# Windowed attention with unscaled probabilities: the softmax reciprocals travel through DRAM and multiply the outputs

## The chip, the core and the metric

The kernel runs on one core of one Trainium2 chip, in one launch. The metric is the device time of a run in microseconds (us), as the median of several runs; smaller is better. One execution was also recorded by the hardware profiler, and everything said of waits and durations comes from that recording. The engines are named as the profile names them: PE is the matrix engine (PEld its weight loads), DVE the vector engine, ACT the scalar engine, POOL the GpSimd engine, SP the engine that issues most of the DMA transfers. An engine works through its own instructions strictly in the order in which they stand; a small q behind a name (SPq) is its queue of issuing and waiting instructions. PSUM is the memory that PE writes its results to; SBUF is the working memory of all engines; DRAM is the large memory outside.

## What is computed

The program is two layers of a diffusion backbone over 512 latent tokens and 256 context tokens, with a model width of 1024. Layer 0 is the windowed attention that the change touches; layer 1 is a retention layer, and both are followed by a gated feed-forward network. Of layer 0, this matters here:

```python
s_ctx = einsum('bqkgd,bnkd->bkgqn', qb, k_c) * scale
s_loc = einsum('bqkgd,bnkd->bkgqn', qb, kb) * scale
s_loc = where(valid, s_loc, NEG_INF)
p = softmax(concatenate([s_ctx, s_loc, sink_col], axis=-1))
o = einsum('bkgqn,bnkd->bqkgd', p[..., :L], v_c) + einsum('bkgqn,bnkd->bqkgd', p[..., L:L + band], vb)
```

There are 16 query heads in 4 groups of 4; the heads of a group share their keys and values. A latent query of a block of 128 sees its own block, the neighbouring blocks and all context keys; a context query sees the 256 context keys. A learned sink logit for each head takes part in the softmax and has no value.

## The kernel before

The stage around the change works in blocks: one group g of four heads, one stream s (0 latent, 1 context) and 128 queries. There are four latent and two context blocks in a group, so 24 in all; the change touches the 18 of groups 0 to 2. They are counted here from 0 to 17 in the order in which the kernel writes them. In each of groups 0 and 1 the four latent blocks come first and then the two context blocks; in group 2 the two context blocks are the third and the sixth. So blocks 4, 5, 10, 11, 14 and 17 are context blocks. A context block has two tiles of 128 keys; a latent block has four (at the ends) or five.

A block goes through these steps:

- `score`, lines 685 to 729, for each of the four heads: PE multiplies queries and keys into PSUM (L710); DVE adds the mask, takes the running minimum and writes the result to an SBUF tile `pr` (L711). After each second head, DVE makes the bias (L717), ACT takes the two exponentials and gets their row sums beside them (L725 is the next step; the exponentials go through the helper at L101), and DVE takes the reciprocals of the two sums (L721). Then the probabilities are scaled by the reciprocals: of each pair, the first head on DVE (L727), the second on ACT (L725).
- `turn`, line 731: for each tile of keys PE transposes the four heads' probabilities into one PSUM bank (L736), and ACT or DVE in turn copies the bank to an SBUF tile `tt` (L738).
- `output`, line 743: PE multiplies values and `tt` (L750) into a PSUM bank, of which the block uses 256 columns: the two halves of the 128 partitions hold two heads each. For groups 0 to 2, DVE copies this result into an SBUF tile `res` (L765), and later work splits it into the two parts that the output projection reads. For group 3 the split reads the bank directly.

In the layout of the scores a query is a partition, and its sum is one number for each partition: a scaling along the free dimension is one operand. In the layout of the outputs a query is a column, and a partition is a channel of the head.

Between the blocks stand pieces of other work. `make_q(j)` (lines 559 to 639) projects the queries of heads 2j and 2j+1: 24 matmuls with 512 columns and 24 with 256 (L147 to L149), then norms (L617 and L620), rotations on DVE (L589 to L592), and for j from 2 to 6 eight DMAs on SP that spread the result over the partitions (L605). It is called after the second and the fourth block of groups 0 to 2, for the next group. The weights come in with DMAs on SP (L122) and are split by ACT (L164) and DVE (L165).

The order on each engine in this stage isn't written by hand. The program is handed to a scheduler, which plays it through with its own estimates of durations, DMAs included, and fixes an order on each engine, SP among them. So the changed source gives a changed order over the whole stage, and the order can be read from the built program before it has run. Where a tile's buffer is used again, the scheduler adds a wait for the earlier use.

Of the kernel before, what the change touches and what calls it, by code (L numbers as in the profile page):

```python
# [8 lines left out]
F32 = mybir.dt.float32  # L9
# [5 lines left out]
P = 128  # L15
# [6 lines left out]
NKV = 4  # L22
# [27 lines left out]
def dit_kernel(ctx, tc, xT, cT, crow, small, consts, masks, tabs0, tabs1, jtab, adaQ, adaN, adaT, wst, out):  # L50
    nc = tc.nc
    mult, add, sub = ALU.mult, ALU.add, ALU.subtract
# [6 lines left out]
    rp = ctx.enter_context(tc.tile_pool(name="rp", bufs=1, reuse_waits="tile"))  # L59
    psJ = ctx.enter_context(tc.tile_pool(name="psJ", bufs=1, reuse_waits="tile", space=PSUM))  # L60

    def T(pool, cols, tag, bufs, dt=F32):
        return pool.tile([P, cols], dt, tag=tag, bufs=bufs, name=tag)
# [36 lines left out]
    def lnexp(*args, **kw):  # L100
        ins = nc.scalar.activation(*args, **kw)  # L101
        after(ins, [turn["pre"]])
        turn["lnexp"].append(ins)
        return ins
# [58 lines left out]
    def split(t, hi, lo, behind=()):  # L163
        after(nc.scalar.copy(hi, t), behind)  # L164
        return nc.vector.tensor_tensor(lo, t, hi, op=sub)  # L165
# [66 lines left out]
    def h_tiles(s):  # L232
        hi = t_h(s)
        if s == 0:
            return hi, t_h(s)
        return hi[:, 0:SC], hi[:, SC:2 * SC]
# [47 lines left out]
    pO = lambda: T(psA, 512, "pO", 1)  # L284
# [234 lines left out]
    At = ExitStack()  # L519
    ap = At.enter_context(tc.tile_pool(name="ap", bufs=1, reuse_waits="tile"))  # L520
# [36 lines left out]
    q, stats = {}, {}  # L557
# [110 lines left out]
    psA2 = At.enter_context(tc.tile_pool(name="psA2", bufs=1, reuse_waits="tile", space=PSUM))  # L668
    pS = lambda: T(psA2, 512, "S2", 3)

    run_dep = mybir.DependencyInfo(mybir.DependencyClass.Sync, mybir.DependencyReason.DATA)
    o_raw = {}
    o_t = [[None] * KT, [None] * KT]

    class Block:


        def __init__(self, g, s, b):
            self.g, self.s, self.b = g, s, b
            self.lk = list(range(max(0, b - 1), min(4, b + 2))) if s == 0 else []  # L680
            ck = [4, 5]
            self.keys = ck + self.lk if s == 0 and b == 3 else self.lk + ck
            self.pr = []

        def score(self, i):
            g, s, b, n = self.g, self.s, self.b, len(self.keys) * P
            hd, nl = 4 * g + i, len(self.lk) * P
            if i % 2 == 0:
                self.st = T(ap, 16, "stat", 4)
            st, c = self.st, 2 * (b + 4 * s)  # L690
            qt = q[hd, s][:, b * P:(b + 1) * P]
            pt = T(ap, 656, "pr", PRB)[:, :n + 1]
            top = stats[hd][:, 1, c + hd % 2:c + hd % 2 + 1]
            nc.gpsimd.tensor_copy(pt[:, n:n + 1], top)
            lo, x0 = st[:, i % 2:i % 2 + 1], self.lk[0] * P if nl else 0

            if nl == 384:
                runs = [(nl, SC, 5 * P, [(0, SC, kc)]), (0, nl, 2 * P, [(0, nl, kx)])]
            elif nl == 0:
                runs = [(0, SC, 5 * P, [(0, SC, kc)])]  # L700
            elif b == 0:
                runs = [(0, n, 3 * P, [(0, nl, kx), (nl, SC, kc)])]
            else:
                runs = [(0, n, 0, [(0, SC, kc), (SC, nl, kx)])]
            for c0, w, m0, parts in runs:
                bank = pS()[:, :w]
                for p0, pw, kk in parts:
                    for r in range(2):
                        keys = kk[g][r] if kk is kc else kk[g][r][:, x0:x0 + pw]
                        nc.tensor.matmul(bank[:, p0:p0 + pw], qt, keys, start=r == 0, stop=r == 1)  # L710
                nc.vector.tensor_tensor_reduce(pt[:, c0:c0 + w], bank, mask[:, m0:m0 + w], 1.0, top, add, ALU.min, lo)  # L711
                top = lo
            self.pr.append(pt)
            if i % 2 == 0:
                return
            y = stats[hd][:, 0, c:c + 2]
            nc.vector.scalar_tensor_tensor(st[:, 2:4], st[:, 0:2], -1.0, y, mult, mult)  # L717
            for e in range(2):
                pt = self.pr[i - 1 + e]
                lnexp(pt, pt, AF.Exp, scale=y[:, e:e + 1], bias=st[:, 2 + e:3 + e], accum_out=st[:, 4 + e:5 + e])  # L720
            nc.vector.reciprocal(st[:, 6:8], st[:, 4:6])  # L721
            for e in range(2):
                pt = self.pr[i - 1 + e]
                if e:
                    nc.scalar.activation(pt[:, :n], pt[:, :n], AF.Identity, scale=st[:, 6 + e:7 + e])  # L725
                else:
                    nc.vector.tensor_scalar(pt[:, :n], pt[:, :n], st[:, 6 + e:7 + e], None, op0=mult)  # L727
            if i == 3:
                self.tt = []
# [12 lines left out]

        def output(self):
            g, s, b = self.g, self.s, self.b
            O = pO()[:, :256]
            for ki, (t, tt) in enumerate(zip(self.keys, self.tt)):
                vg = vt[t][:, g * HD:(g + 1) * HD]
                f, l = ki == 0, ki == len(self.keys) - 1
                for e in range(2):
                    ins = nc.tensor.matmul(O[64 * e:64 * e + 64, :], vg, tt[:, 256 * e:256 * e + 256], start=f, stop=l)  # L750
                    if f:
                        tc.add_manual_dep(ins.ins, self.last.ins.name, run_dep, reason="value products in one run")
            if g == NKV - 1:
                if b == 0:
                    for e in range(2):
                        o_t[s][2 * g + e] = h_tiles(s)
                for e in range(2):
                    hi, lo = o_t[s][2 * g + e]
                    cs = slice(b * P, b * P + P)
                    split(O[:, e * P:e * P + P], hi[:, cs], lo[:, cs])  # L760
                return
            if b % 2 == 0:
                o_raw[g, s, b // 2] = T(rp, 512, "res", 12)
            dst = o_raw[g, s, b // 2].rearrange("p (e b q) -> p e b q", e=2, b=2)[:, :, b % 2, :]
            nc.vector.tensor_copy(dst, O.rearrange("p (e q) -> p e q", e=2))  # L765

    def attend(g, s, b):
        blk = Block(g, s, b)
# [377 lines left out]
    for gsz in FFN_GROUPS:  # L1146
        acts = []
        made[:] = 0, gsz
        for i in range(gsz):
            if f < PLAIN:  # L1150
                acts.append(first[f])
                if f == 1:
                    ends.pop(0)()
            else:
                if f == PLAIN:
                    last_sum()
                a, end = seven()
                acts.append(a)
                if f == PLAIN:
                    ends.pop(0)()  # L1160
                if f == 4:
                    cr = cond_rows(fp)
                if f > 3 and (i or f == 6):
                    ada_next(end)
            if i == 0 and prev is not None:
                output(prev, False)
            f += 1
        prev = acts
# [4 lines left out]
    hpool[0] = H.enter_context(tc.tile_pool(name="hR", bufs=1, reuse_waits="tile", side="right"))  # L1173
    wsel[0] = 0
    output(prev, True)
    F.close()
    E.close()
# [24 lines left out]
    def chunk(i, own=False):  # L1202
        raw = T(qw, 1024, "wx", 4) if own else T(rp, 1024, "wraw", 2)
        nc.sync.dma_start(raw, wst[i])
        return raw
# [156 lines left out]
    for hd in range(RH):  # L1362
# [26 lines left out]
        halves = lambda o: enumerate((o[:, 0:SC], o[:, SC:2 * SC]))  # L1389
# [145 lines left out]
        for i in range(2):  # L1535
            g, v = chunk(bg + i), chunk(bv + i)
# [259 lines left out]
    for gsz in FFN_GROUPS:  # L1796
        acts = []
        for i in range(gsz):
            if f < 2:
                acts.append(first[f])  # L1800
            elif f == 2:
                w = [next_w(fp, behind=norm_end) for _ in range(2)]
                token_sums(hm, 3, sh2, sA, [weights_end])
                other_parts()
                acts.append(plain(w))
            else:
                acts.append(seven(late))
            late = output(prev, False) if i == 0 and prev is not None else ()
            f += 1
        prev = acts  # L1810
# [146 lines left out]
```

## Time and profile before

| | us |
|---|---|
| median of 3 runs (1734.84 to 1737.31) | 1736.23 |
| the profiled execution's own time | 1732.25 |
| its span, first to last instruction | 1730.3 |
| first and last matmul of the scores (L710), from the span's start | 99.5 and 301.8 |
| first and last copy of an output to `res` (L765) | 119.6 and 268.8 |

The profile's page has the busy time of each engine, the span in slices, the chain of work that ended last (followed back from the last instruction, at each step to what released it), groups of equal instructions, and the DMAs. A row of a group says how often it occurs, its busy time and its mean, and the idle time of its engine just before it with what ended that idle time. A row of the stretches gives the busy time of every engine in a part of the span. A row of the timeline gives start, duration, engine, line, operation, and the tiles written and read. A busy PE isn't a PE at its peak, because matmuls overlap each other.

### The profile page before, as it was taken

The page shows a single profiled execution, that of the slowest core. Times are in us where ns is not written, and L with a number is a line of the kernel's source. Part 1 is how long each engine was busy: PE and PEld are TensorE (multiplying, and loading weights), DVE is VectorE, ACT ScalarE, POOL GpSimd, SP SyncE. Part 2 cuts the span into 40 slices and gives each one's busy share as a digit, 9 for nine tenths or more (in the row PEclk, how much of TensorE's full clock was granted, in tenths as well). Part 3 has the DMA queues.
Part 4 walks back from the last instruction along what each step waited for, and adds up shares of the span by engine and source line. Part 5 has one row for each costly group of instructions (what it writes and reads, how often), then busy time and mean ns, then how long its engine had stood idle before and what let it go on. Part 6 is the DMA issues. An engine that isn't in the chain of part 4 may idle for free.

```text
span 1730.3 us, 27786 instructions
## 1 busy us (share of the span) xinstructions
PE 1698.0 (98%) x10876; PEld 1513.0 (87%) x10876; DVE 1361.0 (79%) x2436; ACT 871.1 (50%) x1552; POOL 50.5 (3%) x168
## 2 busy tenths in 40 slices
PE   7999999999999999999999999999999999999999
PEld 5788877899999999999988788898897899899998
DVE  6698889798778788787889858858758798877874
ACT  5587779465433334342556534524525464445442
POOL 0000000000000000000000000000000000000000
PEclk9999999999999999999999999999999999999999
DMA  9612221543253434343423524523423223333322
GB/s 349 239 30 57 62 62 56 209 134 121 73 157 117 153 110 148 123 154 102 156 99 88 183 77 132 163 82 124 159 90 108 95 74 103 117 102 116 100 86 86
DMA packets 62803, 207.48 MB, mean 120 GB/s; under 512 B 7248, under 2 KB 8912, under 8 KB 62416
## 3 DMA queue, kind: packets, MB, share of 16 engines
q1 hardware_dynamic: 55184, 178.97, 32.0%
q0 software_dynamic: 7200, 26.22, 5.2%
q8 instruction: 85, 1.39, 0.3%
q10 hardware_dynamic: 288, 0.52, 0.1%
q14 instruction: 46, 0.38, 0.1%
HBM read 199.65 MB, written 2.10 MB: 117 GB/s over the span
## 4 chain that ended last, share of the span: by engine, by line
PE 78%; DVE 11%; DMA 6%; ACT 3%; issue 2%; SPq 0%; ACTq 0%; DVEq 0%
PE Y L897 14%; PE pj L147 7%; PE Z L897 7%; PE pj L149 7%; PE pj L148 7%; PE Z L1292 6%; PE X L897 3%; DMA wraw<-in_wst_dram 3%; PE pT L736 2%; PE pO L750 2%; PE S L710 2%; DVE wlo L165 2%; PE Y L1281 2%; PE pj L1292 2%; PE X L1281 1%
## 5 line engine op out<-in xcount | busy, mean ns | idle before, releaser
L164 ACT CAST whi<-wraw 128x1024 fp32r<-128x1024 f32 x258 | 270.0, 1051 | 333.7 <-PE Z L149 81.9
L165 DVE TENSOR_TENSOR wlo<-wraw,whi 128x1024 fp32r<-128x1024 f32 x258 | 314.3, 1221 | 64.5 <-ACT whi L164 62.7
L897 PE MATMUL Y<-aq,whi 128*128 128x384 f32 x640 | 173.5, 335 | 0.6 <-ACT hn L1053 0.6
L897 PEld LDWEIGHTS Y<-aq,whi 128*128 128x128 f32 x640 | 116.6, 188 | 1.6 <-ACT hn L1053 1.4
L256 DVE SCALAR_TENSOR_TENSOR res<-pj,mod,res 128x512 f32<-128x512 f32 (+1 forms) x112 | 81.0, 728 | 41.5 <-PE pj L149 41.2
L897 PE MATMUL Y<-aq,wlo 128*128 128x384 f32 x320 | 107.0, 334 | 0.0
L273 DVE CUSTOM_DVE_ANT_0 y<-adaw,crow,small_sb 128x1024 bf16<-128x1024 f32 x64 | 81.9, 1280 | 29.6 <-DMA adaw<-in_adaT_dram 29.4
L1292 PE MATMUL Z<-whi,sA 128*128 128x512 f32 x256 | 81.7, 394 | 1.4 <-ACT gate L1478 1.4
L101 ACT ACTIVATE pr<-pr,stat,qs 128x513 f32<-128x513 f32 (+2 forms) x96 | 74.2, 775 | 9.1 <-DVE stat L717 8.8
L147 PE MATMUL pj<-ax,whi 128*128 128x512 f32 x176 | 69.0, 392 | 1.2 <-DVE res L256 1.2
L149 PE MATMUL pj<-ax,whi 128*128 128x512 f32 x176 | 68.6, 390 | 0.0
L148 PE MATMUL pj<-ax,wlo 128*128 128x512 f32 x176 | 68.6, 390 | 0.0
L147 PE MATMUL pj<-act,whi 128*128 128x512 f32 x168 | 65.6, 391 | 0.0
L148 PE MATMUL pj<-act,wlo 128*128 128x512 f32 x168 | 65.5, 390 | 0.0
L149 PE MATMUL pj<-act,whi 128*128 128x512 f32 x168 | 65.5, 391 | 0.0
L897 PEld LDWEIGHTS Y<-aq,wlo 128*128 128x128 f32 x320 | 60.1, 188 | 0.0
L1292 PEld LDWEIGHTS Z<-whi,sA 128*128 128x128 f32 x256 | 48.0, 188 | 13.0 <-ACT gate L1478 2.6
L711 DVE CUSTOM_DVE_ANT_0 pr<-S,mask,qs 128x256 f32<-128x256 f32 (+1 forms) x96 | 53.1, 566 | 7.8 <-PE S L710 5.3
L897 PE MATMUL Y<-sA,whi 128*128 128x256 f32 x304 | 58.1, 277 | 0.6 <-ACT res L1746 0.6
L897 PE MATMUL Y<-hx,whi 128*128 128x256 f32 x304 | 56.3, 277 | 0.0
L736 PE MATMUL pT<-const_sb,pr 128*128 128x128 f32 x352 | 53.6, 278 | 1.5 <-ACT tt L738 0.9
L1292 PE MATMUL Z<-wlo,sA 128*128 128x512 f32 x128 | 50.7, 396 | 0.2
(581 smaller groups left out, 5070.4 us busy)
## 6 DMA issues: line engine op xcount, KB each, us to landing
wraw<-in_wst_dram SPq DMA_DIRECT2D x224, 512.0 KB, 3.6
adaw<-in_adaT_dram POOLq DMA_DIRECT2D x48, 512.0 KB, 3.9
wx<-in_wst_dram SPq DMA_DIRECT2D x30, 512.0 KB, 4.3
adan<-in_adaQ_dram SPq DMA_DIRECT2D x16, 512.0 KB, 8.8
adan<-in_adaN_dram SPq DMA_DIRECT2D x12, 512.0 KB, 7.7
adaw<-in_adaT_dram SPq DMA_DIRECT2D x8, 512.0 KB, 3.9
res<-in_xT_dram SPq DMA_DIRECT2D x14, 256.0 KB, 3.2
aq<-in_adaN_dram SPq DMA_DIRECT2D x12, 256.0 KB, 5.7
```

The source lines that it names most:

```text
L101: ins = nc.scalar.activation(*args, **kw)
L147: nc.tensor.matmul(o, whi, xhi, start=first, stop=False)
L148: nc.tensor.matmul(o, wlo, xhi, start=False, stop=False)
L149: return nc.tensor.matmul(o, whi, xlo, start=False, stop=last)
L164: after(nc.scalar.copy(hi, t), behind)
L165: return nc.vector.tensor_tensor(lo, t, hi, op=sub)
L256: return nc.vector.scalar_tensor_tensor(res[d], o, mods[l, s][:, part, d:d + 1], res[d], mult, add)
L273: res.append(nc.vector.tensor_tensor_reduce(junk, w, cr[:, s * 1024:(s + 1) * 1024], 1.0, sm_t[:, C_ADAB + l * 48 + j:C_ADAB + l * 48 + j ...
L711: nc.vector.tensor_tensor_reduce(pt[:, c0:c0 + w], bank, mask[:, m0:m0 + w], 1.0, top, add, ALU.min, lo)
L736: nc.tensor.transpose(tp[:, a * P:(a + 1) * P], self.pr[(0, 2, 1, 3)[a]][:, ki * P:(ki + 1) * P], ident)
L897: nc.tensor.matmul(o, p, r, start=first and k + i == 0, stop=k == 3 and i == 2, skip_group_check=not first)
L1292: ins = nc.tensor.matmul(os[t], p, r, start=first and k + i == 0, stop=k == 3 and i == 2, skip_group_check=by_k or not first)
```

## The change

For groups 0 to 2 the probabilities stay unscaled. The two reciprocals of each pair of heads are written by a DMA on SP from the `stat` tile (128 partitions with two numbers each) to a tile of two rows in DRAM: 256 pieces of four bytes. When the second pair of a block has been written, two more DMAs on SP read each row, of 256 numbers, to 64 partitions each: a tile `factor` with a row for every partition. Its buffer alternates between a new one and one that stood unused in this stage (`y1`). The copy of the block's output (L765 before) becomes a product with `factor` (L781 after). The outputs of all blocks now share one PSUM bank, taken once, and blocks of groups 0 to 2 use its two halves in turn. Group 3 is computed as before.

```diff
+    o_bank, o_count = pO(), [0]
+    rows = At.enter_context(tc.tile_pool(name="rows", bufs=1, reuse_waits="tile", space=bass.MemoryType.DRAM))
...
+            self.factor = None
+            if g < NKV - 1:
+                self.row = rows.tile([2, 256], F32, tag="row", bufs=4, name="row")
...
             nc.vector.reciprocal(st[:, 6:8], st[:, 4:6])
+            if g < NKV - 1:
+                nc.sync.dma_start(self.row[:, i // 2 * P:(i // 2 + 1) * P].rearrange("e q -> q e"), st[:, 6:8])
+                if i == 3:
+                    o_count[0] += 1
+                    self.factor = T(ap, 256, "factor", 1) if o_count[0] % 2 else T(rp, 256, "y1", 1)
+                    for e in range(2):
+                        nc.sync.dma_start(self.factor[64 * e:64 * e + 64, :], self.row[e:e + 1, :].broadcast_to([64, 256]))
+                    self.tt = []
+                return
             for e in range(2):
...
-            O = pO()[:, :256]
+            c0 = 0 if self.factor is None else 256 * (o_count[0] % 2)
+            O = o_bank[:, c0:c0 + 256]
...
-            nc.vector.tensor_copy(dst, O.rearrange("p (e q) -> p e q", e=2))
+            halves = [t.rearrange("p (e q) -> p e q", e=2) for t in (O, self.factor)]
+            nc.vector.tensor_tensor(dst, *halves, op=mult)
```

In the changed program the lines behind the insertions move: the reciprocal is L726, the writes of the rows are L728, the reads L733, the remaining scaling of group 3 L740 and L742, the transposes L750, the copies to `tt` L752, the value products L765 and the product with `factor` L781.

## The prediction

> **What bounds the kernel now.** The page was read first. The matrix engine is busy nearly throughout, so a saving counts only where PE waits.
>
> ```profile
> span 1730.3 us, 27786 instructions
> PE 1698.0 (98%) x10876; PEld 1513.0 (87%) x10876; DVE 1361.0 (79%) x2436; ACT 871.1 (50%) x1552; POOL 50.5 (3%) x168
> ```
>
> The change works between 112 us (first scaling of the second pair of heads) and 269 us (last copy of an output). I cut that time into three stretches, by what the chain of waits does in them. Each row gives start and end, length, then busy time and count of PE, PEld, DVE, ACT and POOL, the granted clock, and the DMAs.
>
> ```profile
> 112.00:121.00 9.00, 7.92 (x53) 5.46 (x53) 8.77 (x32) 8.11 (x17) 1.01 (x4) 1.00 0.00 0
> 121.00:247.00 126.00, 124.75 (x903) 102.65 (x902) 102.68 (x338) 98.31 (x221) 10.57 (x60) 1.00 0.24 64
> 247.00:265.00 18.00, 13.46 (x91) 10.43 (x93) 14.60 (x51) 13.99 (x36) 0.55 (x4) 0.91 0.11 31
> ```
>
> In the first, DVE is busy for 8.77 of 9 us. In the long middle PE is busy for 124.75 of 126, and DVE and ACT are idle for 23 and 28 us. In the third, PE is busy for only 13.46 of 18, and its clock was 0.91. The chain, cut to the same stretches, agrees:
>
> ```profile
> by line: DVE pr L711 26.7%; DVE tt L738 14.0%; DVE pr L727 9.6%; PE S L710 9.6%; DVE y L589 8.1%; DVE hn L590 6.7%; DVE y L591 6.7%; DVE hn L592 6.7%; PE pj L617 6.2%; DVE res L765 3.7%; DVE stat L721 0.8%; issue 0.7%; DVE stat L717 0.6%; D
> by line: PE pT L736 20.6%; PE S L710 19.6%; PE pO L750 19.2%; PE pj L147 11.6%; PE pj L149 11.1%; PE pj L148 11.1%; PE pj L617 4.6%; issue 1.2%; ACT tt L738 0.9%; DVE pr L711 0.2%; DVE stat L711 0.2%; DVE hn L165 0.0%; DVEq L711 0.0%
> by line: PE pO L750 20.8%; DVE pr L711 18.5%; ACT pr L101 12.0%; PE S L710 7.3%; DVE q L610 6.2%; PE pT L736 5.5%; issue 4.1%; ACT q L608 3.5%; ACT pr L725 3.4%; PE pj L617 3.1%; ACT qs L101 2.8%; ACT tt L738 2.6%; DVE q L609 2.3%; DVE stat
> ```
>
> DVE sets the first, PE alone the middle, and DVE and ACT in turn the third, where no projections are left to fill PE.
>
> **What is removed.** 36 scalings on DVE and 36 on ACT go (18 blocks, four heads). The groups hold 37 of each, because one pair of group 3 falls into the same time.
>
> ```profile
> L725 ACT ACTIVATE pr<-pr,stat 128x256 f32<-128x256 f32 (+2 forms) x37 | 25.0, 678 | 5.3 <-DVE stat L721 4.4 <-DVE stat L717 0.8
> L727 DVE TENSOR_SCALAR pr<-pr,stat 128x256 f32<-128x256 f32 (+2 forms) x37 | 16.9, 457 | 0.3
> L765 DVE COPY res<-pO 128x256 f32<-128x256 f32 x18 | 7.6, 420 | 4.8 <-PE pO L750 4.7
> ```
>
> That is some 16.5 us of DVE and 24.3 us of ACT, most of it in the middle, where PE covers it. By stretch (length, busy time, count), first the scalings on DVE, then those on ACT:
>
> ```profile
> 112.00:121.00 9.00, 1.05 (x3) 1.00 0.00 0
> 247.00:265.00 18.00, 1.66 (x4) 0.91 0.11 31
> 112.00:121.00 9.00, 1.85 (x3) 1.00 0.00 0
> 247.00:265.00 18.00, 2.42 (x4) 0.91 0.11 31
> ```
>
> First stretch: the chain holds 9.6% of 9 us of L727, 0.87 us; DVE is full, so I take 1.0, with bounds of 0.87 and ACT's 1.85. Third stretch: the chain holds 3.4% of 18 us of L725, 0.6 us; the exponentials queue behind these scalings too, so I take 2.0, between 0.6 and 2.4. Middle: of its chain, 2.5% isn't PE (1.2 + 0.9 + 0.2 + 0.2), 3.1 us; I take 0.7, between 0 and 3.1, since the rows name no scaling there.
>
> **What is moved.** The scheduler's new order moves one costly thing into another place: the split of a weight tile at the head of the third stretch.
>
> ```profile
> 249.48 1.23 DVE L165 TENSOR_TENSOR wlo<-wraw,whi 128x1024 fp32r<-128x1024 f32 x1 [0.28 <-ACT whi L164]
> 254.50 0.47 PE L710 MATMUL S<-kc,q 128*128 128x256 f32 x2 [2.53 <-DVE qs L620]
> 259.48 0.71 ACT L725 ACTIVATE pr<-pr,stat 128x512 f32<-128x512 f32 x1
> 259.85 0.85 PE L736 MATMUL pT<-const_sb,pr 128*128 128x128 f32 x6 [0.47 <-DVE pr L727]
> ```
>
> It stood ahead of the chain that PE awaits for 2.53 us; now it stands behind that, between a reciprocal and a copy to `tt`, where it delays something else by the same 1.23 us. The clock row (0.91 of 18 us) says that up to 1.6 us of PE time went to a lowered clock there. I take a gain of 0.5, between 0 and 1.6. Sum of gains: 1.0 + 2.0 + 0.7 + 0.5 = 4.2 us; bounds 1.5 and 9.0.
>
> **What is added.** The product in place of the copy reads the same 256 columns of PSUM and one SBUF tile more. No row shows it in that form; it stands between nothing added and the copy's own 0.42 us once more, 18 times, off PE: 0 taken. SP gets 36 writes and 36 reads. Its nearest transfers are those of the queries:
>
> ```profile
> L605 SPq DMA_DIRECT2D q<-y x20: 461/538/598, 120.8 to 233.3; - x20
> L605 SPq DMA_DIRECT2D q<-hn x20: 462/587/1467, 122.1 to 234.6; - x20
> DMA to landing us min/median/max: 1.9/2.3/4.2
> q<-hn SPq DMA_DIRECT2D x10, 64.0 KB, 2.9
> out_dram<-res SPq DMA_DIRECT2D x8, 256.0 KB, 2.0
> ```
>
> An issue holds SP for about 0.55 us, so 72 of them hold it for 40 us of 157, which costs nothing by itself. The path that counts is from a block's second reciprocal to its product: write and landing, then two reads one behind the other: 2.3 + 0.55 + 2.3 = 5.1 us by the medians, 1.9 + 0.55 + 1.9 = 4.4 by the fastest, 4.2 + 0.55 + 4.2 = 9.0 by the slowest. The 64 KB reads are like the row with 2.9; for the write of four-byte pieces I take 2.9 as well: 6.3 us.
>
> What covers it? From the second reciprocal over the scaling to the copy, for blocks 0, 5 and 7:
>
> ```profile
> 112.59 0.16 DVE L721 RECIPROCAL stat<-stat 128x2 f32<-128x2 f32 x1
> 113.58 0.48 DVE L727 TENSOR_SCALAR pr<-pr,stat 128x512 f32<-128x512 f32 x1
> 119.64 0.42 DVE L765 COPY res<-pO 128x256 f32<-128x256 f32 x1
> 157.29 0.16 DVE L721 RECIPROCAL stat<-stat 128x2 f32<-128x2 f32 x1
> 158.29 0.50 ACT L725 ACTIVATE pr<-pr,stat 128x256 f32<-128x256 f32 x1
> 161.97 0.42 DVE L765 COPY res<-pO 128x256 f32<-128x256 f32 x1
> 170.77 0.16 DVE L721 RECIPROCAL stat<-stat 128x2 f32<-128x2 f32 x1
> 171.43 0.55 DVE L727 TENSOR_SCALAR pr<-pr,stat 128x640 f32<-128x640 f32 x1
> 180.71 0.41 DVE L765 COPY res<-pO 128x256 f32<-128x256 f32 x1
> ```
>
> So 6.9, 4.5 and 9.8 us pass, of which the scaling takes 1.0 to 1.3. Without it, latent blocks still have 5.6 to 8.7 us until their value products end, but context blocks only 3.2 to 4.1. The new order helps these: ahead of each product it puts other DVE work, which I counted from the order and these means:
>
> ```profile
> L711 DVE CUSTOM_DVE_ANT_0 pr<-S,mask,qs 128x256 f32<-128x256 f32 (+1 forms) x79 | 43.9, 569 | 6.7 <-PE S L710 5.3 <-POOL pr L694 0.5 <-PE pT L736 0.3
> L738 DVE COPY tt<-pT 128x512 f32<-128x512 f32 x30 | 20.7, 689 | 8.3 <-PE pT L736 8.0
> ```
>
> Block 0 has 6.4 us of it (five score reductions, two copies, three rotations of 0.7 and small ones), context blocks 5.6 to 8.0. The larger of the two covers, over the 18 blocks, is 5.6 to 8.7 us, mean 7.0. At 6.3 us only blocks 10, 11, 12 and 14 fall short, by 2.0 us together; the DVE queue stands for that long, and the score reductions and copies behind it, for which PE waits. DVE's idle time takes up part: I book 0.4, with 0 at 5.1 us. The 9.0 us end is rival B.
>
> **The sum.** 4.2 − 0.4 = 3.8 us less. Against the profiled execution's own 1732.25 us (1.95 around the span) that is 1728.5; the median of the runs stands 4.0 above that execution, so the forecast is 1736.2 − 3.8 = **1732.4 us**.
>
> **Rival A is the forecast; B: the factors come late (slower).** The place is L781 at the head of DVE's queue. From the covers above, a path of 7 us lacks 6.4 us in all 18 blocks, of 8 us 18, of 9 us 35. With half of it reaching PE, the gain of 4.2 is eaten at about 7.2 us; at 9 us the time is 1736.2 + 17.7 − 4.2 = 1750. For it: no row has a write of four-byte pieces, and SP waits in its own queue for each row's landing before the reads. Against it: the copies to `tt` that PE needs first stand ahead of the product in most blocks. The Trainium skill (DMA: Bandwidth & Descriptors, Rules for kernel authors and Specifications) says that a strided last dimension becomes one descriptor per element, and that under 512 bytes the engine reads, changes and writes back; by that rule the write is the slow kind, and B is the likelier for it. No run here shows it yet.
>
> A second mechanism makes B dearer: in the new order the value products of block 5 wait for the product of block 4, although they use different halves of the bank, so a late factor also holds PE directly. The Trainium skill (PSUM — Partial Sum Buffer, PSUM bank collisions raise a hardware error) says that two engines may not use one bank at once, by which two halves of a bank are no double buffer; the order agrees.
>
> **C: no change.** The third stretch is ruled by the exponentials and score reductions themselves, so only the chain's own pieces go (0.87 + 0.6 = 1.5), and the 2.0 us of shortfall reach PE in full: 1736.2 − 1.5 + 2.0 = 1736.7. For it: the chain names little of L725 and nothing in the middle.
>
> **D: the queries come late (slower).** The transfers of the next group's queries stand on SP behind reads that wait for a landing. If each of the five projections that use them is held for a landing and two issues, 2.3 + 1.1 = 3.4 us, and a third of it shows: 1736.2 + 5.7 = 1742 with no gain left. Against it: the order puts these transfers where their sources are only just made.
>
> **How the numbers follow.** A 0.45, B 0.21, C 0.24, D 0.10. The bound of a measurable difference is 0.2%, 3.5 us. A gives faster, C the same, B and D slower: 0.45, 0.24, 0.31. A alone reaches from 1736.2 − 9.0 = 1727 to the edge at 1733; the range adds B's end above and a little for a reordered stage below: 1725 to 1750.
>
> **What would show it.** Right: the first and third stretch shorter by 1 and 2 to 3 us, the middle still filled by PE, L781 without idle time before it. B: idle DVE before L781, ended by the DMA of `factor`, and a landing of `row` over 3.5 us. D: PE waiting at the scores for DMAs of q. C: the third stretch unchanged. The forecast is wrong if the stage's last value product of group 2 doesn't come about 4 us earlier.

## The result, and the profile after

| | median, us | beside the kernel before, us | ratio, 95% interval |
|---|---|---|---|
| changed kernel | 1851.64 (1847.62 to 1852.61) | 1735.86 | 1.0667, 1.0656 to 1.0678 |

The change costs 116 us; the forecast was 1732.4, and the range ended at 1750.

The stage was cut out of both traces, from 95 us to about 3 us behind its last score; two more stretches of equal length follow. The columns are those of the prediction's stretches: start and end, length, then busy time and count of PE, PEld, DVE, ACT and POOL, the granted clock, and the DMAs. First the kernel before, then the changed one.

```profile
95.00:305.00 210.00, 202.21 (x1453) 165.76 (x1454) 178.81 (x585) 170.51 (x389) 15.85 (x94) 0.99 0.20 57
305.00:440.00 135.00, 134.50 (x863) 119.95 (x864) 114.35 (x205) 73.34 (x140) 0.73 (x1) 1.00 0.44 149
440.00:1730.00 1290.00, 1279.23 (x7692) 1163.28 (x7690) 1003.75 (x1490) 576.66 (x929) 32.81 (x61) 1.00 0.37 116
```

```profile
95.00:424.00 329.00, 236.31 (x1462) 190.35 (x1462) 167.08 (x551) 151.96 (x355) 17.38 (x96) 0.82 0.26 44
424.00:559.00 135.00, 134.58 (x864) 120.17 (x861) 114.25 (x206) 73.18 (x138) 0.73 (x1) 1.00 0.44 149
559.00:1849.00 1290.00, 1278.85 (x7689) 1162.10 (x7687) 1003.35 (x1489) 576.33 (x929) 32.74 (x61) 1.00 0.38 116
```

Behind the stage nothing has changed; all of the 119 us between the two traces lies in it. PE has the same work (1453 and 1462 matmuls in the records) but is idle for 92.7 us of it instead of 7.8, and what it does takes 34 us more, at a granted clock of 0.82 instead of 0.99. So the stalls were paid twice here: as idle time, and as slower matmuls behind it. The page of the changed kernel has the same on its first line, 35 us more of PE at 94% of the span:

```profile
PE 1733.0 (94%) x10876; PEld 1537.2 (83%) x10876; DVE 1348.5 (73%) x2400; ACT 851.7 (46%) x1516; POOL 51.6 (3%) x168
```

What was waited for in the stage of the changed kernel (engine and line, what it waited for: us in all, times, longest), first by the engines, then by SP's own queue:

```profile
DVE res L781 <- DMA factor<-row: 47.0, 7, 10.8
PE S L715 <- DVE stat L716: 44.4, 15, 6.6
DVE res L781 <- DMA y<-row: 44.0, 6, 13.8
DVE pr L716 <- DMA row<-stat: 24.7, 5, 6.6
```

```profile
SPq L733 <- DMA row<-stat: 125.6, 22, 9.5
```

Three waits are new. DVE stands 91 us at the product, for a factor in one or the other of its buffers; the score reduction stands 24.7 us, because its `stat` tile is still the source of an unfinished write; SP stands 125.6 us ahead of the reads. All three go back to the landing of `row`. The two DMAs by line, first the writes (L728), then the reads (L733); the durations in the row of a line are those of the issue:

```profile
L728 SPq DMA_DIRECT2D row<-stat x36: 359/420/1887, 106.9 to 375.5; - x36
DMA to landing us min/median/max: 8.1/8.9/13.6
```

```profile
DMA to landing us min/median/max: 2.5/3.8/9.7
```

By the medians the path from a reciprocal to its product is 8.9 + 0.55 + 3.8 = 13.2 us. From the end of a block's second reciprocal to the start of its product the trace has 12.3 to 22.1 us, 16.4 on average, since writes also wait for their turn on SP and products for theirs on DVE. Block 2 in the timeline of DVE, then of SP, then of PE:

```profile
145.92 0.16 DVE L726 RECIPROCAL stat<-stat 128x2 f32<-128x2 f32 x1
...
164.30 0.42 DVE L781 TENSOR_TENSOR res<-pO,factor 128x256 f32<-128x256 f32 x1 [9.76 <-DMA factor<-row]
164.64 0.68 DVE L752 COPY tt<-pT 128x512 f32<-128x512 f32 x1
```

```profile
146.47 1.89 SPq L728 DMA_DIRECT2D row<-stat  x1
...
160.13 1.11 SPq L733 DMA_DIRECT2D factor<-row  x2
```

```profile
151.46 2.38 PE L765 MATMUL pO<-tt,v 128*64 128x256 f32 x20
...
166.58 3.48 PE L765 MATMUL pO<-tt,v 128*64 128x256 f32 x16 [9.46 <-DVE tt L752]
```

The reciprocal ends at 146.08 and the write is issued at 146.47; the reads follow only 13.7 us later, when the row has landed (the slowest landing of the 36; both writes of the next block were issued meanwhile), and the product starts 18.2 us behind the reciprocal. DVE had 9.76 us of nothing to do, and the copy to `tt` that PE needs for its next value products stood behind the product, so PE had nothing to do for 9.46 us. Behind that, 16 matmuls took 3.48 us, where 20 had taken 2.38 us before it: the granted clock was 1.00 from 151.40 to 153.90, and in the stretch of the 16 it was 0.55:

```profile
166.50:170.10 3.60, 3.52 (x17) 1.83 (x18) 0.71 (x2) 0.07 (x1) 0.00 (x0) 0.55 0.59 136
```

That the three waits name the same landing left several theories: that one of them is the cost and the others its shadow, that a queue is the cost and not the landing, or that the new order by itself costs the time.

### The profile page after: what moved, and what is told of

Its sections match the earlier page's. It is cut to its first block, busy times and chain, and to the rows that moved or that the text cites. A ratio compares the mean times of both kernels' runs of the same rounds, so it can differ in the third digit from the quotient of the medians.

```text
span 1849.8 us, 27825 instructions
## 1 busy us (share of the span) xinstructions
PE 1733.0 (94%) x10876; PEld 1537.2 (83%) x10876; DVE 1348.5 (73%) x2400; ACT 851.7 (46%) x1516; POOL 51.6 (3%) x168
## 4 chain that ended last, share of the span: by engine, by line
PE 70%; DMA 14%; DVE 11%; ACT 3%; issue 2%; SPq 1%; DVEq 0%; ACTq 0%
PE Y L913 14%; DMA row<-stat 7%; PE Z L913 7%; PE pj L147 6%; PE pj L148 6%; PE pj L149 6%; PE Z L1308 5%; PE X L913 3%; DMA wraw<-in_wst_dram 3%; DVE wlo L165 2%; PE X L1297 1%; PE Y L1297 1%; PE pO L765 1%; PE X L147 1%; PE pj L1308 1%
## 5 line engine op out<-in xcount | busy, mean ns | idle before, releaser
L750 PE MATMUL pT<-const_sb,pr 128*128 128x128 f32 x352 | 61.2, 298 | 26.7 <-DVE tt L752 25.8
L716 DVE CUSTOM_DVE_ANT_0 pr<-S,mask,qs 128x256 f32<-128x256 f32 (+1 forms) x96 | 53.0, 567 | 33.6 <-DMA row<-stat 24.7
L750 PEld LDWEIGHTS pT<-const_sb,pr 128*128 128x128 f32 x352 | 43.7, 151 | 38.3 <-DVE tt L752 26.7
L765 PE MATMUL pO<-tt,v 128*64 128x256 f32 x352 | 51.6, 442 | 21.1 <-DVE tt L752 17.7
L715 PE MATMUL S<-kc,q 128*128 128x256 f32 x192 | 47.8, 337 | 18.2 <-DVE stat L716 17.7
L715 PE MATMUL S<-k,q 128*128 128x256 f32 (+1 forms) x128 | 37.7, 368 | 26.7 <-DVE stat L716 26.7
L765 PEld LDWEIGHTS pO<-tt,v 128*64 128x64 f32 x352 | 26.7, 158 | 40.5 <-DVE tt L752 19.4
```

The costliest lines, as they stand in the source:

```text
L750: nc.tensor.transpose(tp[:, a * P:(a + 1) * P], self.pr[(0, 2, 1, 3)[a]][:, ki * P:(ki + 1) * P], ident)
```

## The experiments

Every run here is a program of its own, and the scheduler makes a new order for each. In the changed kernel some 11 operations of DVE stand between a block's second reciprocal and its product, in the run without DMAs some 8. What a run is worth therefore holds its own order too.

### The removal, the wait at the product, the reuse of the buffer, and the DMAs by themselves

The run without DMAs:

```diff
+    const_f = T(ap, 256, "factor", 1)
+    nc.gpsimd.memset(const_f, 1.0)
...
-                nc.sync.dma_start(self.row[:, i // 2 * P:(i // 2 + 1) * P].rearrange("e q -> q e"), st[:, 6:8])
...
-                    self.factor = T(ap, 256, "factor", 1) if o_count[0] % 2 else T(rp, 256, "y1", 1)
-                    for e in range(2):
-                        nc.sync.dma_start(self.factor[64 * e:64 * e + 64, :], self.row[e:e + 1, :].broadcast_to([64, 256]))
+                    self.factor = const_f
```

> The removal alone: probabilities unscaled, no row writes and no reads, the product takes a constant tile of ones (so the outputs of groups 0 to 2 stay unscaled). Late factors (the product waits for its DMAs): 1736 less about 4 us, 1727 to 1736, and no idle time of DVE before the product except for PE. The new order or the shared output bank costs the time by itself: 1800 or more, close to the changed kernel's 1852.

Measured: 1729.61, before 1733.37, ratio 0.9981 (0.9973 to 0.9990). A new order and the shared bank by themselves cost nothing; all in all this program gains 3.8 us (by the interval 1.7 to 4.7). The order is this program's own, so that the changed kernel's order costs nothing isn't shown by this run alone. The product, by its line: 425 ns, where the copy had 420.

```profile
L778 DVE TENSOR_TENSOR res<-pO,factor x18: 417/425/426, 116.7 to 263.7; 128x256 f32<-128x256 f32 x18
```

The run with unread factors:

```diff
-            halves = [t.rearrange("p (e q) -> p e q", e=2) for t in (O, self.factor)]
-            nc.vector.tensor_tensor(dst, *halves, op=mult)
+            one = ones.rearrange("p (e q) -> p e q", e=1).broadcast_to([P, 2, P])
+            nc.vector.tensor_tensor(dst, O.rearrange("p (e q) -> p e q", e=2), one, op=mult)
```

> All 72 DMAs stay and are waited for by SP, but the product takes a constant tile of ones and not the factor (the outputs of groups 0 to 2 stay unscaled). Late factors: the 91 us of DVE's idle time before the product go; what stays is at most the 25 us in which the score reduction waits for a row's write to release its buffer, so 1732 to 1757. SP held by its waits (its queue delays other transfers): the time stays near 1852, since every wait of SP is still there.

Measured: 1806.33, ratio 1.0421 (1.0407 to 1.0435), 73 us over the kernel before. That is outside both expectations. The product waits for no DMA any more, and 73 us stay, so DVE's standing there isn't the whole cost; the waits of this run's engines in the stage show what has come up in its place:

```profile
ACT y L164 <- DMA q<-y: 42.0, 5, 10.8
DVE pr L716 <- DMA row<-stat: 27.9, 6, 8.2
DVE hn L165 <- ACT y L164: 25.5, 3, 9.8
```

ACT waits to write the next half of the queries into `y`, because the transfer out of it hasn't run yet: it is the queries' transfers on SP that are late now. So a second theory was formed: each of the three waits is a cost by itself, and the landing is the root of all.

More buffers for the sums:

```diff
-                self.st = T(ap, 16, "stat", 4)
+                self.st = T(ap, 16, "stat", 8)
```

> The changed kernel with eight buffers for the sums' tile instead of four. Late factors: the score reduction no longer waits for a row's write (24.7 us of idle time before), but the factor is as late as it was, so DVE meets a part of that wait at the product instead: 1827 to 1852. If the reuse of the buffer were the main cost: below 1800.

Measured: 1839.84, ratio 1.0616 (1.0600 to 1.0633): some 9 us of the 116, as expected of a wait that is met again at the product.

The DMAs by themselves; the chain behind the last result, cut to its first kind (`z` and `f` are tiles in SBUF, `row` is in DRAM):

```diff
+    def back():
+        nc.sync.dma_start(f[0:64, :], row[0:1, :].broadcast_to([64, 256]))
+        nc.vector.tensor_copy(z[0:64, :], f[0:64, :])
+
+    for _ in range(4):
+        nc.sync.dma_start(row[0:2, 0:P].rearrange("e q -> q e"), z[:, 0:2])
+        back()
```

> The kernel before with small DMAs after its last result, one at a time in a chain, nothing else running (the output is the reference's). Each kind four times: a write to DRAM of 256 numbers in 4-byte pieces from 128 partitions, of 32 numbers in 4-byte pieces, of one number, of 128 pieces of 8 bytes, of 8 pieces of 128 bytes, of 2 of 512 bytes, of one of 1 KB; then writes within SBUF of 2 x 512, 128 x 8 and 64 x 64 bytes; behind each DRAM write the read of a row to 64 partitions. If the four-byte pieces make the write slow: about 8 to 9 us for the first kind, less with fewer pieces, 2 to 3 us for 512 bytes and 1 KB. If it was a busy queue in the changed kernel: about 2 to 3 us for every kind.

SP's timeline in this run has a write and then the read that waits for it. One pair each of 256 pieces of 4 bytes (L1830), 32 pieces of 4 bytes (L1833), 8 of 128 bytes (L1842) and 2 of 512 bytes (L1845):

```profile
1745.19 0.37 SPq L1830 DMA_DIRECT2D zrow<-z  x1
1753.57 0.46 SPq L1826 DMA_DIRECT2D f<-zrow  x1
...
1787.66 0.32 SPq L1833 DMA_DIRECT2D zrow<-z  x1
1788.98 0.46 SPq L1826 DMA_DIRECT2D f<-zrow  x1
...
1848.69 0.29 SPq L1842 DMA_DIRECT2D zrow<-z  x1
1849.86 0.45 SPq L1826 DMA_DIRECT2D f<-zrow  x1
...
1864.86 0.22 SPq L1845 DMA_DIRECT2D zrow<-z  x1
1865.95 0.45 SPq L1826 DMA_DIRECT2D f<-zrow  x1
```

From start to start: 8.4 us (the other three 7.5 to 7.9), 1.3, 1.2 and 1.1 us. Of the kinds not shown, 128 pieces of 8 bytes, side by side and from 128 partitions, took 2.8 to 3.5 us, and a single piece of 4 bytes or of 1 KB took 1.0 to 1.1. With nothing else running the change's write is nearly as slow as in the kernel (8.9 us by the median), so a busy queue explains at most a small part of it. The reads landed in 2.5 us.

### Take the waits apart, and take the slow landing away

The writes alone, on top of the run with unread factors:

```diff
-                    for e in range(2):
-                        nc.sync.dma_start(self.factor[64 * e:64 * e + 64, :], self.row[e:e + 1, :].broadcast_to([64, 256]))
```

> As the run with unread factors, but the 36 reads of the rows are left out too: the 36 writes of four-byte pieces stay, nothing on SP waits for their landing, the product takes a tile of ones (the outputs of groups 0 to 2 stay unscaled). If the 73 us that were left there come from SP standing ahead of the reads until the row has landed, with the transfers of the queries behind it: they go, and only the score reduction's wait for the sums' tile is left, 1730 to 1757. If the slow pieces clog the transfer queue itself, so that the queries' transfers behind them land late whether SP waits or not: 1780 to 1806.

Measured: 1772.32, before 1733.32, ratio 1.0223 (1.0209 to 1.0237): 34 us less than with the reads, but again outside both expectations. The wait for the sums' tile was 30.9 us here, and 39 us were left over the kernel before.

The rows in pieces of 128 bytes (the `stat` tile gets 32 columns, POOL sets it to ones first, the `qs` tile is cut to its 36 used columns to make room, and the transpose turns each block of 32 queries):

```diff
-                nc.sync.dma_start(self.row[:, i // 2 * P:(i // 2 + 1) * P].rearrange("e q -> q e"), st[:, 6:8])
+                rt = T(ap, 32, "rt", 2)
+                nc.vector.transpose(rt, st)
+                for e in range(2):
+                    nc.sync.dma_start(self.row[e:e + 1, i // 2 * P:(i // 2 + 1) * P].rearrange("o (b q) -> (o b) q", q=32),
+                                      rt[6 + e::32, :])
```

> The changed kernel, complete, but the reciprocals are turned into rows by a 32x32-block transpose on DVE (36 of them), and written in pieces of 128 bytes, with two write issues for a pair in place of one (72 instead of 36). The probe had 1.2 us from the issue of such a write to the issue of the read that waits for it, against 7.9 us for the four-byte pieces. If the slow landing is the root of all three waits (product, SP, sums' tile): 1730 to 1742, the 1729.6 of the run without DMAs and up to 12 us for the transposes and the extra issues, and no wait for a factor of over 3 us. If waits of this kind cost by being there, whatever the landing takes: over 1780.

Measured: 1731.62, ratio 0.9990 (0.9981 to 0.9998): the whole loss is gone, and this version is within 0.2% of the kernel before. Its transposes, by line; then, from the line of its reads, the row of SP's waits ahead of them, and who waited for the reads:

```profile
L730 DVE STREAM_TRANSPOSE rt<-stat x36: 195/207/214, 107.8 to 262.8; 128x32 f32<-128x32 f32 x36
```

```profile
L738 SPq EVENT_SEMAPHORE  x36: 17/17/1175, 114.1 to 267.0; - x36
...
  DVE res L786: 0.3, 1
```

SP's longest wait ahead of a read is 1.7 us instead of 9.5 (the longest single row of it 1.2), and the product waited once, for 0.3 us. The waits are all still in the program, and there are 108 issues instead of 72; only the landing is short. (The order is again this program's own.)

The reads on POOL:

```diff
-                        nc.sync.dma_start(self.factor[64 * e:64 * e + 64, :], self.row[e:e + 1, :].broadcast_to([64, 256]))
+                        nc.gpsimd.dma_start(self.factor[64 * e:64 * e + 64, :], self.row[e:e + 1, :].broadcast_to([64, 256]))
```

> The changed kernel, complete, with the 36 reads of the rows issued by POOL instead of SP: SP no longer stands for a landing, the factor comes as late as before. If the late factor ahead of the product is enough by itself: 1800 to 1852, with the idle time of DVE ended by the factor still 60 us or more. If SP's standing was most of it: 1750 to 1790. POOL's own copies behind the waiting reads (the sinks' columns for the score reductions) can add to either.

Measured: 1845.27, ratio 1.0650 (1.0629 to 1.0672). DVE's idle time at the product was 70.8 + 23.8 us. Taking the waits off SP gives nearly nothing by itself, just as taking the wait off the product left 73 us. POOL, with its copies for the score reductions, stood for the landings in SP's place (82.9 + 72.9 us), so this run alone doesn't say that the product's wait is enough; the run with the product's wait alone, below, says more.

### Each wait alone

The writes alone and SP's standing alone, each with eight buffers for the sums' tile (the edit of the `stat` line above on top of the two runs):

> As the run with the writes alone (1772), with eight buffers for the sums' tile instead of four (the outputs of groups 0 to 2 stay unscaled). If what is left there is the score reduction's wait for a row's write to release its buffer (30.9 us of idle time before L716): 1735 to 1745. If the queries' transfers, which landed in 4.2 us instead of 2.3 there, hold the stage by themselves: 1755 to 1772.

> As the run with unread factors (1806), with eight buffers for the sums' tile (the outputs of groups 0 to 2 stay unscaled). If SP's standing for the landing is a cost of its own beside the wait for that buffer: 1765 to 1785, that is 1806 less up to 28, and 30 us or more over the run with the writes alone and eight buffers. If both are the same wait seen twice: equal to that run, 1735 to 1745.

Measured, before at 1732.18: the writes alone 1739.26, ratio 1.0043 (1.0028 to 1.0057); with SP standing 1800.75, ratio 1.0390 (1.0373 to 1.0408). By the ratios, each against the runs of before in its own call, the buffer's wait alone is worth (1.0223 − 1.0043) × 1733 = 31 us. SP's standing is worth 1800.75 − 1739.26 = 61 us; 1800.75 lies above the 1765 to 1785 expected, and the eight buffers took only some 5 us off the run with unread factors. It isn't quite alone: 7.2 us of waiting for the sums' tile are left in this run. SP's timeline shows what happens:

```profile
184.04 1.09 SPq L728 DMA_DIRECT2D row<-stat  x2
193.44 1.09 SPq L733 DMA_DIRECT2D factor<-row  x2
194.57 0.58 SPq L122 DMA_DIRECT2D wraw<-in_wst_dram  x1
195.20 0.94 SPq L728 DMA_DIRECT2D row<-stat  x2
205.16 1.09 SPq L733 DMA_DIRECT2D y<-row  x2
206.34 0.55 SPq L605 DMA_DIRECT2D q<-y  x1
```

```profile
211.57 0.40 ACT L164 CAST y<-hn 128x256 fp32r<-128x256 f32 x1 [18.12 <-DMA q<-y]
```

Two writes, eight to nine microseconds of standing, the reads, the writes of the next block, and again; the first query transfer comes behind two such rounds, at 206.34, and ACT, on its own timeline, waits 18.12 us for it. SP, which had time to spare, now holds ACT.

The queries' transfers on POOL, on top of that:

```diff
-                        nc.sync.dma_start(t[64 * half:64 * half + 64, :].bitcast(F32), src[64 * e:64 * e + 64, :].bitcast(F32))
+                        nc.gpsimd.dma_start(t[64 * half:64 * half + 64, :].bitcast(F32), src[64 * e:64 * e + 64, :].bitcast(F32))
```

> As the run with unread factors and eight buffers (1800.75), but the 40 transfers of the queries are issued by POOL, so they no longer stand behind SP's waits (the outputs of groups 0 to 2 stay unscaled). If the late queries are the way in which SP's standing reaches PE: 1740 to 1760, and ACT's 60.8 us of waiting for the buffer of the queries' halves gone. If it is the weights' loads or the rows themselves: 1780 to 1801.

Measured: 1770.20, before 1733.35, ratio 1.0218 (1.0203 to 1.0234): by the ratios (1.0390 − 1.0218) × 1733 = 30 us less, half of what SP's standing costs; all of it was expected (1740 to 1760). ACT's wait for `y` fell from 60.8 to 10.7 us. What stays is in part the wait for the sums' tile, 20.4 us even with eight buffers, as the writes that free it still stand behind SP's waits; the rest isn't taken apart, and these transfers landed later on POOL (6.5 us by the median, against 3.1).

The product's wait alone:

```diff
-                self.st = T(ap, 16, "stat", 4)
+                self.st = T(ap, 16, "stat", 8)
...
-            nc.gpsimd.tensor_copy(pt[:, n:n + 1], top)
+            nc.vector.tensor_copy(pt[:, n:n + 1], top)
...
-                        nc.sync.dma_start(self.factor[64 * e:64 * e + 64, :], self.row[e:e + 1, :].broadcast_to([64, 256]))
+                        nc.gpsimd.dma_start(self.factor[64 * e:64 * e + 64, :], self.row[e:e + 1, :].broadcast_to([64, 256]))
```

> The changed kernel, complete, with eight buffers for the sums' tile, the reads of the rows on POOL, and POOL's copies of the sinks' columns given to DVE (96 small copies, at most some 10 us of DVE): of the three waits only the product's wait for its factor is left, on DVE. If DVE's standing there is enough by itself: 1780 to 1840, with some 60 to 95 us of idle time ahead of the product. If it needed the other two: 1740 to 1770.

Measured: 1838.89, ratio 1.0605 (1.0587 to 1.0623), 105.5 us over the kernel before. The rows of the product's line that say what ended DVE's idle time ahead of it:

```profile
  DMA factor<-row: 75.7, 9
  DMA y<-row: 24.6, 4
```

100.3 us of standing. The stage of this run, from 95 us to about 3 us behind its last score, says how it shows in the time:

```profile
95.00:412.00 317.00, 230.30 (x1459) 187.49 (x1459) 172.46 (x646) 150.86 (x355) 18.77 (x36) 0.84 0.27 46
```

PE is idle for 86.7 us of it instead of 7.8, 79 us more, and its matmuls take 28 us more, at a granted clock of 0.84. So 79 of the 100.3 us reach PE as idle time, and the slower matmuls make up the rest of the 105.5. The 96 copies given to DVE took 14.0 us of it, not 10, and no run has them without the wait, so their part in the 105 us stays open. With these reservations, alone the three waits cost some 105, 61 and 31 us, and all together 116: they don't add up, since all of them are for the same landings.

### Why the write is slow

> The kernel before with a second chain of small DMAs after its last result (its output is the reference's): writes to DRAM of 4-byte pieces, 256 pieces side by side (as in the change), 128 from 128 partitions, 128 from 64 partitions, 256 at steps of 64 bytes, 256 at steps of 512 bytes, 128 at steps of 512 bytes; 128 pieces of 512 bytes; then reads of 256 4-byte pieces from DRAM. If the slowness is a matter of the count of pieces: about 8 us for all three of 256, half of it for 128. If it is that neighbouring pieces share a line of DRAM and are changed one after the other: about 8 us side by side and 2 us at steps of 512 bytes. For the reads: 2 us, if only writes are slow.

The same kind of chain; SP's timeline, a pair each of 256 pieces side by side (L1836), 128 side by side from 128 partitions (L1839), 256 at steps of 64 bytes (L1845) and 256 at steps of 512 bytes (L1848):

```profile
1757.35 0.36 SPq L1836 DMA_DIRECT2D zrow<-z  x1
1765.18 0.45 SPq L1832 DMA_DIRECT2D f<-zrow  x1
...
1781.91 0.34 SPq L1839 DMA_DIRECT2D zrow<-z  x1
1788.94 0.45 SPq L1832 DMA_DIRECT2D f<-zrow  x1
...
1874.47 0.38 SPq L1845 DMA_DIRECT2D zmid<-z  x1
1876.12 0.45 SPq L1832 DMA_DIRECT2D f<-zmid  x1
...
1891.48 0.37 SPq L1848 DMA_DIRECT2D zwide<-z  x1
1893.04 0.45 SPq L1832 DMA_DIRECT2D f<-zwide  x1
```

7.8, 7.0, 1.7 and 1.6 us. Half as many pieces side by side are hardly faster (7.0 to 7.8 us from 128 partitions, 6.9 to 7.6 from 64), and as many pieces at steps of 64 bytes take a fifth: at these numbers it is lying side by side that costs, not their number. It isn't that alone: the 32 side by side took 1.3 us, and 128 of 8 bytes 2.8 to 3.5. The four reads of 256 pieces of 4 bytes took 2.3 us each, from start to start.

The profile's records of the DMA engines' packets say where the time of a slow write lies. For the one issued at 1745.19 in the first chain, the view of the DMAs has these lines, first from its issue to 1746.4, then from there to 1753.5:

```profile
DMA packets 272, 0.00 MB, mean 1 GB/s; under 512 B 272, under 2 KB 272, under 8 KB 272
DMA packets 0, 0.00 MB, mean 0 GB/s; under 512 B 0, under 2 KB 0, under 8 KB 0
```

All packets are on record 1.2 us after the issue, and then for 7.1 us there is none, until the row has landed. The write at steps of 64 bytes (1874.47) has the same 272 packets in the same 1.2 us. So what is slow isn't the handling of many small pieces by the DMA engines, but what comes between the last packet and the landing; no record shows what that is.

## Why the prediction was wrong, by its steps

**What bounds the kernel, and the gains: right in the sum, in part by luck.** 4.2 us were forecast for the removal; without the DMAs the kernel gains 3.8. The first product came at 116.7 instead of 119.6, of which 1.1 lies ahead of the stage (its first score at 98.4 instead of 99.5): 1.8 us in the first stretch, where 1.0 was booked. From the first to the last product it is 147.0 us instead of 149.2: 2.2, where 2.0 + 0.7 + 0.5 was booked. The 1.1 us ahead of the stage stand in no term. The stage's last score ends that trace 4.2 us earlier. The product at nothing more than the copy was right as well (425 and 420 ns).

**The step that failed: the path from the second reciprocal to the product.** "for the write of four-byte pieces I take 2.9 as well: 6.3 us", with 9.0 as the slow end. The write's landing was taken from rows of transfers of whole rows of 256 numbers and more, and so was its upper end. It measured 8.9, the path 13.2. The rest of that step holds: with the covers' mean of 7.0 us, a path of 13.2 lacks 18 × 6.2 = 112 us, and the run with the product's wait alone had 100.3 us of standing. A bound from the nearest row is no bound where the new thing differs from that row in kind; "no row has a write of four-byte pieces" stood in the text, and still the range ended at the slowest landing of the nearest row, 4.2 us.

**"half of it reaching PE": too little.** With 100.3 us of standing PE was idle for 79 us more, and its matmuls took 28 us more: some 105 us in the time, with the copies on DVE among their causes. What is added has no term for the lowered clock.

**72 issues, "which costs nothing by itself": right of the issues, wrong of the queue.** 108 of them cost nothing with a short landing. But a read stands on SP for its row, and SP's standing costs 61 us where the product doesn't wait. That is rival D's place: the queries behind the reads. D priced it at 2.3 + 1.1 us for each projection and a third showing, 5.7 in all; the queries' part is about 30 us. The late transfers were foreseen rightly, and the landing is the same mis-sized term. But with 8.9 us in it D would have had 5 × (8.9 + 1.1) / 3 = 16.7 us, so the third showing was too little as well; and it isn't PE that waits at the scores for a DMA of `q`, as D's sign has it, but ACT for the buffer `y` (13.1 us in the changed kernel, 60.8 with the product's wait gone and eight buffers).

**Not in any step: the sums' tile.** The write reads `stat`, so the tile is free only when the write has landed; 24.7 us of waiting in the changed kernel, 31 us of time where nothing else waits.

**The rivals.** B's place, L781 at the head of DVE's queue, was right, and its test came out as written (idle DVE ended by the DMA of `factor`, a landing over 3.5 us). Its time of 1750 failed with the 9.0 us. B's second mechanism, value products held by the bank's two halves, hardly showed: the product's line in the changed kernel has PE waiting 3.5 us for it. C and D as whole outcomes are out.

**What made B the likelier.** The Trainium skill's sentence (DMA: Bandwidth & Descriptors, Rules for kernel authors and Specifications) made B the likelier, and of the direction it was right: the element-wise write took 8.9 us. Neither of its parts is what decided here: 256 pieces of 4 bytes at steps of 64 bytes, as element-wise as the change's, took 1.6 us; pieces of 128 bytes took 1.2 us in the probe, and those of 512 bytes 1.1.

## What to carry to other kernels

When a value goes from a column (one number for each partition) to a row through DRAM, turn it on an engine first and write it in long pieces: here 36 transposes of 0.207 us on DVE took the ratio from 1.0667 to 0.9990. (Even so the change is worth no more than 0.2%: the scalings it removes stood beside a busy PE.) Price an operation that the trace doesn't show by measuring it alone, in a chain behind the last result, before anything is built on it. And follow a slow landing to all who hold something for it: the engine that uses the data, the queue that stands ahead of the next transfer, and the buffer that is the transfer's source; here freeing one of them gained 3, 9 and 43 of the 116 us, as long as the others stood.

## What the runs showed of the hardware

- Writes to DRAM of 4-byte pieces side by side from 128 partitions: 7.0 to 8.4 us in the chains, for 128 as for 256 pieces; the same 256 at steps of 64 or 512 bytes 1.6 to 2.1 us, 32 pieces side by side from 16 partitions 1.3 us, 128 pieces of 8 bytes side by side 2.8 to 3.5 us. The packets of the slow write are all on record 1.2 us after its issue, and the landing follows 7 us later. The expectation's idea that neighbours are changed one after the other agrees with the steps, but not with the 32, which are neighbours too; it stays open.
- Transfers beside the slow writes land later: those of the queries took 4.2 us by the median in the run with the writes alone, against 2.3 in the kernel before and 2.2 in the run without DMAs.
- The granted clock was lower in the run with the stalls: 0.82 over the 329 us of the stage against 0.99, and 34 us more of PE's busy time for the same matmuls. Behind one stall of 9.46 us it was 0.55 for 3.6 us.
